# One tap of the feed-forward's convolution scaled by ScalarE and added two tiles at a time, in a hybrid decoder layer

## The chip, the cores and the metric

The kernel runs on one core of one Trainium2 chip. The metric is the device time of one execution in microseconds (us); the time before is the median of three runs. Engines are named as in the profile: PE is TensorE (PEld its weight loads), DVE is VectorE, ACT is ScalarE, POOL is GpSimd, SP issues most DMAs.

## The reference

One decoder layer over 256 tokens and 2048 features, all in float32. Two mixers run side by side on the normed input: a chunked retention with 8 heads, and a gated linear recurrence behind a causal convolution. Their gated sum goes through a projection into the residual stream. Cross-attention to 256 memory tokens (4 heads of 512) follows, then the part that the change touches, and a last norm:

```python
def conv_gated_ffn(hn, w_up, conv_w, conv_b, w_down):
    up = causal_dwconv(hn @ w_up, conv_w, conv_b)      # 3 taps along the tokens, per feature
    gate, val = jnp.split(up, 2, axis=-1)              # 2 x 5632 features
    return (jax.nn.silu(gate) * val) @ w_down
...
        hn = rmsnorm(h, norm_ffn_w[l])
        h = h + conv_gated_ffn(hn, ffn_w_up[l], ffn_conv_w[l], ffn_conv_b[l], ffn_w_down[l])
    return rmsnorm(h, final_norm_w)
```

The convolution is causal: feature by feature, `y[s] = w2*x[s] + w1*x[s-1] + w0*x[s-2] + bias`.

## The kernel before, in words

**Products.** Each float32 product is made of three products of a shorter type (`F32R`): the left side `h + l` and the right side `hi + lo` give `h*hi + l*hi + h*lo`. Weights stream from memory in chunks, in one order for the whole kernel (`weight_plan`, `weight_stream`). ScalarE casts each chunk to `hi` (L451), VectorE subtracts to get `lo` (L452), two chunks ahead of TensorE (`AHEAD = 2`), into rings of six tiles each. L285 is the one line that issues all matmuls.

**Pairs.** `steps_pair` multiplies 256 tokens by two blocks of 512 columns at once, one k-pair (2 x 128 features) per chunk. Two row tiles, two column blocks and two k-tiles make eight products of 512 columns, of three matmuls each. For a k-pair that is *marked* seven products do, after a scheme that multiplies sums of blocks: sums of the weights (`seven_parts`, L473, on VectorE), sums of the token blocks (`sums_of`), and, after the last marked k-pair, a recombination on VectorE (L627) and ScalarE (L620), with three last adds at the pair's end (L638). A pair with no mark is not paired: `weight_plan` turns it into two ordinary products (`gemm_n`).

**MARKS** lists, for each stage and each pair in it, the marked k-pairs. A number below 10 is a marked k-pair whose sums VectorE makes. A number above 20 (22 stands for k-pair 2) is a marked one of which some sums are loaded: `load_twice` brings one block into both halves of a tile `tw`, and `add_to` lets POOL issue a DMA that accumulates two more blocks onto it; VectorE makes two adds that are left (L337). A negative number is no mark: it names a k-pair whose `lo` is made by DMA (tiles `fr` and `fl`; -1 the whole, -11 half of k-pair 1). 

**Order of the work.** Engines work in their own order; a scheduler places instructions, those under `tc.high_priority` early. Work that is to lie beside later products is put off with `later(n, fn)`: `fn` is issued after `n + 1` more chunks. `LAG` holds these numbers by name: `gate` and `value` (the chunks between the end of an up-projection block and its convolution), `key_turn` (the chunks until transposed keys are joined), `sum_load` and `sum_add` (how many chunks ahead the two parts of a loaded sum are issued), `residual` (squares for the norm), `gelu`, `rnn`, `heads`, `squares`, `two_heads` and others. `by_rotate`, `by_conv`, `by_gelu` and `by_attend` choose ScalarE (not 0) or VectorE (0) for the scaling of rows in `turned_rows`.

**The feed-forward.** 11 blocks (0 to 10) of 512 gate and 512 value features: each is a pair of `ffn_w_up` with the gate's and the value's columns. Down-projections stand between them after blocks 4 and 8 and at the end (`ff_plan`). A block's two results are scaled by row on ScalarE (L1421), split into 16-bit planes (L664), transposed by DMA, joined by ScalarE (L677) and then given to `conv` (gate) or `conv` and `gate_up` (value), half of the block's tiles (`pr` 0 or 1) per chunk. `conv` handles a tile of 128 features x 256 tokens: tap 2 and the bias on ScalarE (L1280), taps 1 and 0 as one multiply-add each on VectorE (L1282). `gate_up` applies SiLU (L1290), multiplies (L1291) and splits the result for the down-projection.

Of the kernel before, what the change touches and what calls it, by code (L numbers as in the profile page):

```python
# [13 lines left out]
AF = mybir.ActivationFunctionType  # L14
ALU = mybir.AluOpType
AX = mybir.AxisListType

P = 128
D = 2048
S = 256  # L20
NT = D // P
# [5 lines left out]
FF = 5632  # L27
NF = FF // P
BW = 512
# [5 lines left out]
WARM = 7  # L35
FREE = 300
LAG = dict(
    sums=3, two_heads=3, recur=3, gelu=6, merged=4, memory=1, memory_step=4, rnn=2, rnn_step=2,
    heads=2, heads_step=1, squares=2, squares_step=1, rows=17, rows_step=2, residual=5, gate=2,
    value=4, merge_turn=1, query_turn=2, key_turn=3, turn=3, attend=3, acc_m=0, acc_h=0,  # L40
    by_rotate=0, by_conv=0, by_gelu=1, by_attend=1, far=0, far_load=3, sum_load=4, sum_add=0,
)
EPS = 1e-6
GN_EPS = 1e-5
FF_PARTS = [4, 4, 3]
EARLY = [2, 2, 4, 4, 4]
MARKS = [
# [9 lines left out]
]  # L57

O_Q, O_K, O_V, O_G = 0, 1024, 2048, 4096
O_XR, O_YR, O_GA, O_GB = 6144, 8192, 10240, 12288  # L60
# [139 lines left out]
def hybrid_layer(  # L200
# [17 lines left out]
    act, dve, pe, pool, sp = nc.scalar, nc.vector, nc.tensor, nc.gpsimd, nc.sync  # L218
# [11 lines left out]
    def nm(s):  # L230
        count[0] += 1
        return f"{s}_{count[0]}"

    def big(shape, dt=F32, s="b"):
        return bp.tile(shape, dt, tag="big", name=nm(s))

    def tmp(s="t"):
        return tp.tile([P, 2, S], F32, tag="tmp", name=nm(s))
# [30 lines left out]
    pf = cp.tile([P, 4, NF2], F32, name="pf")  # L269
# [28 lines left out]
    at, scale0, split, far = [0], [], [], {}  # L298
# [181 lines left out]
    def later(n, fn):  # L480

        pending.append((step[0] + n + 1, fn))
# [18 lines left out]
    def ended(steps):  # L501

        for a in steps:
            pass
        return a
# [34 lines left out]
    def gemm_n(*args):  # L540
        return ended(steps_n(*args))
# [98 lines left out]
    def pair(*args):  # L640
        return ended(steps_pair(*args))

    def paired():

        return isinstance(plan[gemms[0]][3], tuple)
# [42 lines left out]
    def turned_rows(a, r, then, wait=1, urgent=True, by=0):  # L688

        rows = big([P, 2, BW], s="rows")  # L690
        with tc.high_priority(FREE) if urgent else nullcontext():
            for tt in range(2):
                scale = act.mul if by else dve.tensor_scalar_mul
                scale(rows[:, tt, :], a[:, tt, :], r[:, tt : tt + 1])  # L694
        by_dma(rows, then, wait)
# [15 lines left out]
    def split_rows(a, r):  # L711

        hi, lo = (big([P, 2, BW], F32R, s="v") for _ in range(2))
        for tt in range(2):
            c = r[:, tt : tt + 1]
            act.mul(hi[:, tt, :], a[:, tt, :], c)
            dve.scalar_tensor_tensor(
                out=lo[:, tt, :], in0=a[:, tt, :], scalar=c, in1=hi[:, tt, :].bitcast(F32),
                op0=ALU.mult, op1=ALU.subtract,
            )  # L720
        return hi, lo
# [78 lines left out]
    xs = Pairs(x_t, p_mix, 1)  # L800
# [9 lines left out]
    rs0 = rstd_rows(ss0)  # L810
# [115 lines left out]
    for g in range(2):  # L926
        dec = big([P, 4, S], s="dec")
        vs, turned = [], ([], [])
        for b, o in enumerate((O_Q, O_K)):

            def rotate_both(f, o=turned[b]):
                o.append(rotated(f[:, 0:2, :]))
                later(0, lambda: o.append(rotated(f[:, 2:4, :])))

            v = None
            if b and not g and paired():
                a, v = pair("w_in", 0, xs, NT, O_K, O_V + BW)
                scaled(a, rs0)
                by_dma(a, rotate_both)
            else:  # L940
                a = gemm_n("w_in", 0, xs, NT, o + g * BW) if g + b else q0
                turned_rows(a, rs0, rotate_both, 2 - b if g + b else 3, g + b > 0, LAG["by_rotate"])
            if b == 1:
                sp.dma_start(
                    out=dec,
                    in_=consts[:, C_DEC + g * 4 * S : C_DEC + (g + 1) * 4 * S].rearrange("p (h s) -> p h s", s=S),
                )
            if g == 0:
                if v is None:
                    v = gemm_n("w_in", 0, xs, NT, O_V + b * BW) if b else ended(v_steps)  # L950
                vs.append(split_rows(v, rs0))
        if g == 1:
            vs += [split_rows(v, rs0) for v in pair("w_in", 0, xs, NT, O_V + 1024, O_V + 1024 + BW)]
        qr, kr = turned
        gates = []
        c = O_G + g * 1024
        for a in pair("w_in", 0, xs, NT, c, c + BW):
            t = big([P, 2, BW], s="gate")
            for tt in range(2):
                act.activation(t[:, tt, :], a[:, tt, :], AF.Silu, scale=rs0[:, tt : tt + 1])  # L960
            gates.append(t)
        retain(g, qr, kr, vs, dec, gates)
# [30 lines left out]
    rnn = []  # L993
# [83 lines left out]
    def tanh_rows(t, a):  # L1077
        for tt in range(2):
            act.activation(t[:, tt, :], a[:, tt, :], AF.Tanh, scale=half_rs0[:, tt : tt + 1])
        return t  # L1080
# [4 lines left out]
    merged, rsms, hrow = [], [], []  # L1085
# [14 lines left out]
    def turn_merged(f):  # L1100
        for pr in range(2):
# [6 lines left out]
            if len(merged) == 2:  # L1108
                for k2 in range(NT // 2):
                    later(LAG["memory"] + LAG["memory_step"] * k2, lambda k2=k2: ms[k2])  # L1110

    ts, mb = [], []
    for b in range(2):
        ts.append(tanh_rows(big([P, 2, BW], s="sig"), gemm_n("w_in", 0, xs, NT, O_GB + b * BW)))
# [2 lines left out]
                later(LAG["rnn"] + LAG["rnn_step"] * i, lambda k2=k2: sums_of(rnn[k2]))  # L1117
    for b in (0, 2):
        if b:
            ts = [tanh_rows(a, a) for a in pair("w_in", 0, xs, NT, O_GB + b * BW, O_GB + (b + 1) * BW)]  # L1120
        for t, z in zip(ts, pair("w_proj_rnn", 0, rnn, NT, b * BW, (b + 1) * BW)):
            gated(t, z)
            mb.append(z)
# [3 lines left out]
        later(LAG["squares"] + LAG["squares_step"] * c, lambda c=c: memory_squares(c))  # L1127
    ts = []
    for b in (0, 2):
        ts += [tanh_rows(a, a) for a in pair("w_in", 0, xs, NT, O_GA + b * BW, O_GA + (b + 1) * BW)]  # L1130
    later(3, memory_begun)
    for b in range(4):
        later(LAG["rows"] + LAG["rows_step"] * b, lambda b=b: hrow.append(load_rows(x, b)))
# [123 lines left out]
    for b, a in enumerate(pair("xa_w_v", 0, ms, NT, 0, BW)):  # L1257
        v = split_rows(a, rsms[0])
        later(LAG["attend"] + b, lambda b=b, v=v: attend(b, v))
    attention(2)  # L1260
    if paired():
        for b, a in enumerate(pair("xa_w_v", 0, ms, NT, 2 * BW, 3 * BW)):
            v = split_rows(a, rsms[0])
            later(LAG["attend"] + b, lambda b=b, v=v: attend(2 + b, v))
    else:
        for b in (2, 3):
            v = split_rows(gemm_n("xa_w_v", 0, ms, NT, b * BW), rsms[0])
            later(1, lambda b=b, v=v: attend(b, v))

    h2s = []  # L1270
    ss2 = residual("xa_w_o", osp, h2s, p_ffn, marks_of("ffn_w_up"))
    rs2 = rstd_rows(ss2)


    def conv(z, t0, dst, pr):

        for j in (2 * pr, 2 * pr + 1):
            t = t0 + j
            y = dst[:, j, :]
            act.activation(y, z[:, j, :], AF.Identity, scale=pf[:, 2, t : t + 1], bias=pf[:, 3, t : t + 1])  # L1280
            for s in range(1, 3):
                dve.scalar_tensor_tensor(  # L1282
                    out=y[:, s:S], in0=z[:, j, 0 : S - s], scalar=pf[:, 2 - s, t : t + 1], in1=y[:, s:S],
                    op0=ALU.mult, op1=ALU.add,
                )

    def gate_up(gt, vl, hid, seven, pr):
        cs = slice(2 * pr, 2 * pr + 2)
# [14 lines left out]
    def down(b0, hid, n):  # L1303

        for b in (0, 2):
            for i, z in enumerate(pair("ffn_w_down", b0 * BW, hid, n, b * BW, (b + 1) * BW)):
                pool.dma_start(out=hrow[b + i], in_=z, accum_op=ALU.add)

    def down_final(b0, hid, n):
# [85 lines left out]
    def up(b, hid, seven, wait):  # L1395

        gt, vl = (big([P, 4, S], s=a) for a in ("fg", "fv"))

        def by_two(fn):
            fn(0)  # L1400
            if b < NF // 4 - 1:
                later(0, lambda: fn(1))
            else:
                fn(1)

        def gate(f):
            by_two(lambda pr: conv(f, 4 * b, gt, pr))

        def value(f):

            def both(pr):
                conv(f, NF + 4 * b, vl, pr)
                gate_up(gt, vl, hid, seven, pr)

            by_two(both)

        two = pair("ffn_w_up", 0, h2s, NT, b * BW, FF + b * BW)
        for a, then, wait in zip(two, (gate, value), (LAG["gate"], wait)):
            with tc.high_priority(FREE):
                for tt in range(2):  # L1420
                    act.mul(a[:, tt, :], a[:, tt, :], rs2[:, tt : tt + 1])  # L1421
            by_dma(a, then, wait)

    hid = {}
    for kind, b, *n in ff_plan():
        if kind == "up":
            b0 = max(one[1] for one in ff_plan() if one[0] == "down" and one[1] <= b)
# [3 lines left out]
        else:  # L1431
            final = b + n[0] == NF // 4
            if final:
                wfin = []
                for i in range(2):
                    t = big([P, 2, BW], s="wf")
                    sp.dma_start(
                        out=t.rearrange("p a n -> p (a n)"),
# [42 lines left out]
```

## Time and profile before

| | us |
|---|---|
| median of three runs | 1955.75 (1953.15 to 1957.33) |
| profiled execution, its own time | 1956.59 |
| its span, first to last instruction | 1954.5 |
| TensorE busy | 1944.4 (99%) |
| VectorE busy | 1659.0 (85%) |
| ScalarE busy | 1457.7 (75%) |
| casts to `hi`, L451 (824) | 801.1 |
| subtractions to `lo`, L452 (824) | 940.4 |

The granted clock of TensorE was 0.999. TensorE's bars overlap, since a matmul's bar (0.39 us for 512 columns) is longer than the distance to the next (0.23 us), and their ends are modelled. The pace is better read from the chain of work that ended last, which lists stretches with their number of matmuls.

### The profile page before, as it was taken

To read this page: it belongs to the slowest core of one execution; us is meant where nothing else is said; L and a number is where in the kernel's file an instruction comes from. 1 tells how busy PE (TensorE), PEld (TensorE's weight loads), DVE (VectorE), ACT (ScalarE), POOL (GpSimd) and SP (SyncE) were. 2 spreads that over 40 slices of the span, in tenths; PEclk is the share of its full clock that TensorE was granted. 3 is DMA by queue.
4 is the path that set the end of the run, shared out by engine and by line. 5 is a ranking of instruction groups with operands and counts; after the bars stand their busy time and mean duration, and the time that the engine had idled before them with its cause. 6 is when DMAs were issued, how large, how long until landed. Compare 5 with 4: busy or idle time off the path is not lost.

```text
span 1954.5 us, 24287 instructions
## 1 busy us (share of the span) xinstructions
PE 1944.4 (99%) x8735; PEld 1612.9 (83%) x8735; DVE 1659.0 (85%) x2155; ACT 1457.7 (75%) x1792; POOL 68.5 (4%) x69
## 2 busy tenths in 40 slices
PE   9999999999999999999999999999999999999998
PEld 7888888888888888888888888888887888888887
DVE  6887987787889988887888857789999889999986
ACT  6665758999756666778678777888877578884784
POOL 0000001000100000000000000000000000000000
PEclk9999999999999999999999999999999999999999
DMA  8866767666867786778868687676677877678773
GB/s 332 262 215 198 245 222 217 213 218 229 237 217 265 233 264 215 253 253 252 247 213 239 223 221 225 226 232 226 211 224 224 269 248 221 223 224 271 230 255 119
DMA packets 211352, 454.99 MB, mean 233 GB/s; under 512 B 143264, under 2 KB 147872, under 8 KB 170400
## 3 DMA queue, kind: packets, MB, share of 16 engines
q1 hardware_dynamic: 204896, 430.38, 66.5%
q0 software_dynamic: 6336, 23.07, 6.3%
q8 instruction: 68, 1.11, 0.2%
q14 instruction: 52, 0.43, 0.1%
HBM read 407.27 MB, written 2.10 MB: 209 GB/s over the span
## 4 chain that ended last, share of the span: by engine, by line
PE 88%; DVE 5%; ACT 3%; DMA 2%; issue 2%; POOL 0%; SPq 0%; POOLq 0%; DVEq 0%; ACTq 0%
PE acc L285 63%; PE sm L285 26%; DVE lo L452 2%; ACT hi L451 1%; DMA raw<-in_wall 1%; ACT f L677 1%; DVE o L627 1%; ACT pl L664 0%; DMA fl<-fr 0%; DVE o L638 0%; DMA pt<-pl 0%; DVE raw L473 0%; DVE fv L1282 0%; DVE fg L1282 0%; DVE s L702 0%
## 5 line engine op out<-in xcount | busy, mean ns | idle before, releaser
L452 DVE TENSOR_TENSOR lo<-raw,hi 128x1024 fp32r<-128x1024 f32 (+1 forms) x824 | 940.4, 1169 | 203.0 <-ACT hi L451 193.0
L285 PE MATMUL acc<-hi,s 128*128 128x512 f32 x3526 | 1081.5, 388 | 0.4 <-ACT s L727 0.2
L451 ACT CAST hi<-raw 128x1024 fp32r<-128x1024 f32 (+1 forms) x824 | 801.1, 1007 | 301.9 <-DMA raw<-in_wall 83.1
L285 PEld LDWEIGHTS acc<-hi,s 128*128 128x128 f32 x3526 | 659.5, 188 | 136.1 <-DVE s L728 0.6
L285 PE MATMUL acc<-lo,s 128*128 128x512 f32 x1727 | 669.7, 388 | 0.1
L285 PE MATMUL sm<-hi,s 128*128 128x512 f32 x1464 | 450.9, 389 | 0.0
L285 PEld LDWEIGHTS acc<-lo,s 128*128 128x128 f32 x1727 | 324.4, 188 | 68.6 <-DVE lo L452 2.1
L285 PEld LDWEIGHTS sm<-hi,s 128*128 128x128 f32 x1464 | 274.7, 188 | 57.2 <-ACT prob L1203 0.2
L285 PE MATMUL sm<-lo,s 128*128 128x512 f32 x720 | 280.3, 389 | 0.0
L677 ACT COPY f<-pt 128x1024 uint16<-128x1024 uint16 x128 | 166.8, 1353 | 10.0 <-DMA pt<-pl 10.0
L285 PEld LDWEIGHTS sm<-lo,s 128*128 128x128 f32 x720 | 135.2, 188 | 28.6 <-DVE lo L452 0.6
L285 PE MATMUL acc<-hi,ts 128*128 128x512 f32 x438 | 134.9, 389 | 0.0
L473 DVE TENSOR_TENSOR raw<-raw 128x1024 f32<-128x1024 f32 x147 | 127.1, 865 | 1.9
L285 PEld LDWEIGHTS acc<-hi,ts 128*128 128x128 f32 x438 | 82.2, 188 | 17.0
L285 PE MATMUL acc<-lo,ts 128*128 128x512 f32 x219 | 85.7, 391 | 0.7 <-DVE lo L452 0.6
L664 ACT COPY pl<-o 128x1024 uint16<-128x1024 uint16 x64 | 62.5, 1040 | 3.7 <-DVE o L638 2.8
L330 POOL DMA_DIRECT2D tw<-in_wall x24 | 21.4, 891 | 980.8 <-DMA tw<-in_wall 355.7
L285 PEld LDWEIGHTS acc<-lo,ts 128*128 128x128 f32 x219 | 41.1, 188 | 10.8 <-DVE lo L452 2.4
L664 ACT COPY pl<-rows 128x1024 uint16<-128x1024 uint16 x44 | 43.7, 1044 | 7.6 <-DVE rows L694 7.6
L1421 ACT ACTIVATE o<-o,ro 128x512 f32<-128x512 f32 x44 | 30.1, 718 | 23.9 <-DVE o L638 23.8
L638 DVE TENSOR_TENSOR o<-o,sm 128x512 f32<-128x512 f32 x64 | 42.2, 679 | 3.9 <-PE sm L285 3.9
L285 PE MATMUL sm<-hi,ts 128*128 128x512 f32 x146 | 45.0, 389 | 0.0
(197 smaller groups left out, 1321.2 us busy)
## 6 DMA issues: line engine op xcount, KB each, us to landing
raw<-in_wall SPq DMA_DIRECT2D x319, 1024.0 KB, 5.1
raw<-in_wall SPq DMA_DIRECT2D x24, 768.0 KB, 5.6
tw<-in_wall SPq DMA_DIRECT2D x24, 512.0 KB, 7.7
tw<-in_wall POOLq DMA_DIRECT2D x24, 512.0 KB, 7.3
raw<-in_wall SPq DMA_DIRECT2D x13, 512.0 KB, 6.6
fr<-in_wall SPq DMA_DIRECT2D x12, 512.0 KB, 7.4
fl<-fr POOLq DMA_DIRECT2D x12, 512.0 KB, 8.1
nat<-in_x SPq DMA_DIRECT2D x8, 512.0 KB, 9.7
```

Of the source, the lines that this page charges most:

```text
L285: tc.keep_in_program_order(pe.matmul(*a, **k))
L330: pool.dma_start(out=far[i], in_=source(i)[:, 0:KH, :], accum_op=ALU.add)
L451: act.copy(hi[:, cs], src[:, cs])
L452: dve.tensor_tensor(out=lo[:, cs], in0=src[:, cs], in1=hi[:, cs].bitcast(F32), op=ALU.subtract)
L473: dve.tensor_tensor(out=o, in0=a, in1=b, op=ALU.add)
L627: dve.tensor_tensor(out=o, in0=a, in1=b, op=op)
L638: dve.tensor_tensor(out=o, in0=o, in1=a, op=ALU.add)
L664: act.copy(planes[:, tt], words[:, tt])
L677: act.copy(halves_[:, :, :, cs], turned_[:, :, :, cs])
L1421: act.mul(a[:, tt, :], a[:, tt, :], rs2[:, tt : tt + 1])
```

## The change

In `conv`, tap 1 is no longer a multiply-add on VectorE. ScalarE scales each tile by tap 1 into a temporary tile `fu`, and one add on VectorE over two tiles (510 elements) puts it, shifted by one token, onto the result. Tap 0 stays a multiply-add.

A helper `blocks` stands where `pair` stood in some places, and yields either a pair's results or those of two ordinary products, so that a pair without marks works there too. It is used where block 10 of the up-projection has no marks now; its rows then go through `turned_rows` (`by_up=0`: VectorE scales).

The marks are set anew: 70 marked k-pairs in place of 73, of which 28 in place of 24 have sums by DMA; three of the halves by DMA (-15 and one -11 in the first recurrent projection, where k-pair 1 is now marked, and -17) are gone. Delays are set anew as well; `sum_add=1` issues the accumulating DMA one chunk earlier.

```diff
 LAG = dict(
-    sums=3, two_heads=3, recur=3, gelu=6, merged=4, memory=1, memory_step=4, rnn=2, rnn_step=2,
-    heads=2, heads_step=1, squares=2, squares_step=1, rows=17, rows_step=2, residual=5, gate=2,
-    value=4, merge_turn=1, query_turn=2, key_turn=3, turn=3, attend=3, acc_m=0, acc_h=0,
-    by_rotate=0, by_conv=0, by_gelu=1, by_attend=1, far=0, far_load=3, sum_load=4, sum_add=0,
+    sums=3, two_heads=2, recur=3, gelu=7, merged=4, memory=1, memory_step=4, rnn=3, rnn_step=1,
+    heads=3, heads_step=2, squares=1, squares_step=0, rows=17, rows_step=2, residual=2, gate=2,
+    value=4, merge_turn=1, query_turn=2, key_turn=5, turn=3, attend=3, acc_m=0, acc_h=0,
+    by_rotate=0, by_conv=0, by_gelu=0, by_attend=4, far=0, far_load=3, sum_load=4, sum_add=1,
+    by_up=0,
 )
 MARKS = [
-    ((), (3, 24, 26), (23,), (3, 4, 26, -11),),
-    ((22, 23, 24, -16, -15, -11), (2, 5, 6, -17, -11), (2, 3, 5),),
-    ((5, 6, 22), (22, 25, 26), (3, 25, 26), (5,),),
+    ((), (3, 24, 26), (23,), (23, 24, 26, -11),),
+    ((1, 22, 24, -16), (2, 5, 6, -11), (22, 23, 25),),
+    ((5, 6, 22), (22, 25, 26), (3, 5, 26), (5,),),
     ((3,), (3, 5),),
-    ((), (5, 23, -6), (2, 3), (2, 5), (2, 5, 23, -1), (),),
+    ((), (5, 23, -6), (2, 3), (2, 5), (22, 23, 25, -1), (),),
     ((22, 25, 26), (),),
     ((2, 4), (2, 5, -1), (3,), (2, 5), (2, 5), (5, 22), (4, 5),),
-    ((3, 22, 24), (2, 5), (4, 22), (4, 5), (2, 5), (4, 22),),
-    ((2, 3, 4, 6), (2, 24), (),),
+    ((2, 23, 24), (2, 5), (22,), (4, 5), (2, 5), (4, 22),),
+    ((2, 3, 4, 6), (), (),),
 ]
@@
+    def blocks(w, row, st, nk, c1, c2):
+
+        if paired():
+            yield from ((a, True) for a in pair(w, row, st, nk, c1, c2))
+        else:
+            for c in (c1, c2):
+                yield gemm_n(w, row, st, nk, c), False
+
@@
     def conv(z, t0, dst, pr):
 
+        cs = slice(2 * pr, 2 * pr + 2)
+        one = tmp("fu")
         for j in (2 * pr, 2 * pr + 1):
             t = t0 + j
-            y = dst[:, j, :]
-            act.activation(y, z[:, j, :], AF.Identity, scale=pf[:, 2, t : t + 1], bias=pf[:, 3, t : t + 1])
-            for s in range(1, 3):
-                dve.scalar_tensor_tensor(
-                    out=y[:, s:S], in0=z[:, j, 0 : S - s], scalar=pf[:, 2 - s, t : t + 1], in1=y[:, s:S],
-                    op0=ALU.mult, op1=ALU.add,
-                )
+            act.activation(
+                dst[:, j, :], z[:, j, :], AF.Identity, scale=pf[:, 2, t : t + 1], bias=pf[:, 3, t : t + 1]
+            )
+            act.mul(one[:, j - 2 * pr, :], z[:, j, :], pf[:, 1, t : t + 1])
+            dve.scalar_tensor_tensor(
+                out=dst[:, j, 2:S], in0=z[:, j, 0 : S - 2], scalar=pf[:, 0, t : t + 1], in1=dst[:, j, 2:S],
+                op0=ALU.mult, op1=ALU.add,
+            )
+        dve.tensor_tensor(out=dst[:, cs, 1:S], in0=one[:, :, 0 : S - 1], in1=dst[:, cs, 1:S], op=ALU.add)
@@
-        two = pair("ffn_w_up", 0, h2s, NT, b * BW, FF + b * BW)
-        for a, then, wait in zip(two, (gate, value), (LAG["gate"], wait)):
+        two = blocks("ffn_w_up", 0, h2s, NT, b * BW, FF + b * BW)
+        for (a, own), then, wait in zip(two, (gate, value), (LAG["gate"], wait)):
+            if not own:
+                turned_rows(a, rs2, then, wait, by=LAG["by_up"])
+                continue
             with tc.high_priority(FREE):
```

Left out above: other places where `pair` becomes `blocks`, all of which keep their pairs.

More of the change, by code (lines that the diff above doesn't have):

```diff
@@ L952, in hybrid_layer @@
         if g == 1:
-            vs += [split_rows(v, rs0) for v in pair("w_in", 0, xs, NT, O_V + 1024, O_V + 1024 + BW)]
+            vs += [split_rows(v, rs0) for v, _ in blocks("w_in", 0, xs, NT, O_V + 1024, O_V + 1024 + BW)]
         qr, kr = turned
@@ L956, in hybrid_layer @@
         c = O_G + g * 1024
-        for a in pair("w_in", 0, xs, NT, c, c + BW):
+        for a, _ in blocks("w_in", 0, xs, NT, c, c + BW):
             t = big([P, 2, BW], s="gate")
@@ L1110, in turn_merged, with tanhs @@
                     later(LAG["memory"] + LAG["memory_step"] * k2, lambda k2=k2: ms[k2])
+    def tanhs(c):
+        for a, own in blocks("w_in", 0, xs, NT, c, c + BW):
+            yield tanh_rows(a if own else big([P, 2, BW], s="sig"), a)
     ts, mb = [], []
@@ L1119, in hybrid_layer @@
         if b:
-            ts = [tanh_rows(a, a) for a in pair("w_in", 0, xs, NT, O_GB + b * BW, O_GB + (b + 1) * BW)]
+            ts = list(tanhs(O_GB + b * BW))
         for t, z in zip(ts, pair("w_proj_rnn", 0, rnn, NT, b * BW, (b + 1) * BW)):
@@ L1129, in hybrid_layer @@
     for b in (0, 2):
-        ts += [tanh_rows(a, a) for a in pair("w_in", 0, xs, NT, O_GA + b * BW, O_GA + (b + 1) * BW)]
+        ts += tanhs(O_GA + b * BW)
     later(3, memory_begun)
@@ L1305, in down @@
         for b in (0, 2):
-            for i, z in enumerate(pair("ffn_w_down", b0 * BW, hid, n, b * BW, (b + 1) * BW)):
+            for i, (z, own) in enumerate(blocks("ffn_w_down", b0 * BW, hid, n, b * BW, (b + 1) * BW)):
+                if not own:
+                    a, z = z, big([P, 2, BW], s="o")
+                    with tc.high_priority(FREE):
+                        act.copy(z, a)
                 pool.dma_start(out=hrow[b + i], in_=z, accum_op=ALU.add)
@@ L1415, in value @@
             by_two(both)
-        two = pair("ffn_w_up", 0, h2s, NT, b * BW, FF + b * BW)
-        for a, then, wait in zip(two, (gate, value), (LAG["gate"], wait)):
+        two = blocks("ffn_w_up", 0, h2s, NT, b * BW, FF + b * BW)
+        for (a, own), then, wait in zip(two, (gate, value), (LAG["gate"], wait)):
+            if not own:
+                turned_rows(a, rs2, then, wait, by=LAG["by_up"])
+                continue
             with tc.high_priority(FREE):
```

## The prediction

> **What bounds the kernel now.** I read the page first, then the waits of TensorE and of its weight loads, then the chain of waits in order of time.
>
> ```profile
> span 1954.5 us, 24287 instructions
> PE 1944.4 (99%) x8735; PEld 1612.9 (83%) x8735; DVE 1659.0 (85%) x2155; ACT 1457.7 (75%) x1792; POOL 68.5 (4%) x69
> ...
> PE acc L285 <- DMA fl<-fr: 0.6, 1, 0.6
> ...
> PEld acc L285 <- DVE lo L452: 4.6, 11, 0.8
> ...
> PEld acc L285 <- DMA fl<-fr: 1.1, 1, 1.1
> ...
> 220.49 5.44 PE sm L285 x24
> ...
> 251.09 6.12 PE acc L285 x27
> ```
>
> TensorE is busy for 1944.4 of 1954.5 us, and a busy bar that is modelled could hide gaps, so the chain decides: 24 matmuls of 512 columns take 5.44 us and 27 take 6.12, both 0.2267 us each, in pieces 30 us apart. Products follow one another at one pace. What interrupts them is small: weight loads waited 4.6 us for `lo` (11 times, at most 0.8) and 1.1 once for a remainder that a DMA makes. So two things move the time: the number of products, and whether the parts of the weights (`hi` cast by ScalarE, `lo` subtracted by VectorE) are there in time. The reserve behind that is thin, which the stretches with the feed-forward's convolution show:
>
> ```profile
> core 0: us, PE busy (x) PEld busy (x) DVE busy (x) ACT busy (x) POOL busy (x), PEclk, DMA share, GB/s
> 1290.00:1503.00 213.00, 212.53 (x933) 174.33 (x932) 195.40 (x269) 181.43 (x224) 0.89 (x1) 1.00 0.69 216
> 1588.00:1756.00 168.00, 168.00 (x743) 139.16 (x742) 156.10 (x213) 145.47 (x179) 1.77 (x2) 1.00 0.73 224
> ```
>
> The first holds five blocks of some 42 us, the second four. VectorE is at 92% and 93%, ScalarE at 85% and 87%. TensorE sets the pace; VectorE is close behind it and ScalarE third.
>
> **The sum's base.** The profiled execution took 1956.59 us (span 1954.5 and 2.1 around it), 0.84 above the median of 1955.75. I sum against 1956.59 and take 0.84 off at the end.
>
> **Fewer seven-product k-pairs: +2.04 us.** A k-pair of a paired product takes 24 matmuls (the 24 of the chain's row), and 21 when it is marked, since one of eight products in three parts each goes. Counting the marks, positive ones only, gives 73 before and 70 after: block 7 of the up-projection loses one and block 10 both of its two, which makes it unpaired. That is 3 x 3 = 9 matmuls more, 9 x 0.2267 = 2.04 us, all on the bounding engine. An unpaired product has as many matmuls as a pair without marks. No cover exists for this term.
>
> **The one DMA wait that goes: -0.8 us.** In the first projection of the recurrent branch the marks -15 and -11 go, and k-pair 1 becomes a plain marked one. The wait stood at its first `fl`:
>
> ```profile
> 511.20 0.62 PE L285 MATMUL sm<-hi,s 128*128 128x512 f32 x2
> ...
> 511.88 0.61 PE L285 MATMUL acc<-hi,s 128*128 128x512 f32 x2
> 513.12 0.50 PE L285 MATMUL acc<-fl,s 128*128 128x512 f32 x1 [0.63 <-DMA fl<-fr]
> ```
>
> Two matmuls that follow at pace end 0.62 us after the first began, so one lasts 0.39 and starts 0.23 after the last: 0.16 of it overlaps. The idle 0.63 therefore cost 0.63 + 0.16 = 0.8. What is late next there is k-pair 1's sums and parts on VectorE; I take nothing for it, since the casts are made two chunks ahead, and bound it at 0.8 lost again.
>
> **Work that VectorE and ScalarE trade outside the convolution: 0.** These are the durations:
>
> ```profile
> L452 DVE TENSOR_TENSOR lo<-raw,hi 128x1024 fp32r<-128x1024 f32 x745 | 889.4, 1220 | 199.5 <-ACT hi L451 189.7 <-PE acc L285 4.2 <-PE sm L285 2.1
> L451 ACT CAST hi<-raw 128x1024 fp32r<-128x1024 f32 x745 | 755.4, 1048 | 273.3 <-DMA raw<-in_wall 80.5 <-PE acc L285 60.6 <-DVE raw L473 45.0
> ...
> L473 DVE TENSOR_TENSOR raw<-raw 128x512 f32<-128x512 f32 x98 | 67.3, 687 | 1.4
> ...
> L473 DVE TENSOR_TENSOR raw<-raw 128x1024 f32<-128x1024 f32 x49 | 59.8, 1219 | 0.5
> ...
> L337 DVE TENSOR_TENSOR raw<-tw,raw 128x512 f32<-128x512 f32 x24 | 16.4, 684 | 0.2
> ...
> L561 ACT CAST ts<-tq 128x512 fp32r<-128x512 f32 x35 | 21.7, 620 | 19.2 <-DVE tq L559 19.1
> ```
>
> A marked k-pair whose sums VectorE makes costs it 1.219 + 2 x 0.687 = 2.59 us of adds. With a sum by DMA two adds of 0.684 stay, 1.37, so each of the sums that becomes a DMA's (24 to 28) frees 1.22, and costs two more transfers of 512 KB, off the path while they land in time. The accumulating transfers are also issued one chunk, 5.44 us, earlier, on POOL's queue, where a marked k-pair now gets its data sooner. Three far halves fewer (a remainder by DMA) put 1.22 each back on VectorE. These edits relieve a VectorE that is not late at most of their places. Their cover is the 42 us of matmuls of each block; if it goes, the price is at most the 4.6 us that weight loads waited for `lo`. A gain has the same bound. I take 0. The moved scalings (`by_gelu`, `by_up`) and the other delays move tens of small operations under the same cover: 0, with the delay of the keys priced below.
>
> **The convolution's tap: +3.9 us.** Per block of the up-projection (8 row tiles, 11 blocks) VectorE ran 16 multiply-adds; now 8 of them and 4 adds over two tiles, and ScalarE runs 8 scalings more.
>
> ```profile
> L1282 DVE SCALAR_TENSOR_TENSOR fg<-f,pf,fg 128x255 f32<-128x255 f32 x44 | 20.4, 479 | 3.1 <-ACT fg L1280 3.0
> ...
> 1482.34 1.66 DVE L1282 SCALAR_TENSOR_TENSOR fg<-f,pf,fg 128x255 f32<-128x255 f32 x4
> ...
> L1291 DVE TENSOR_TENSOR fo<-ft,fv 128x512 f32<-128x512 f32 x22 | 15.0, 682 | 0.0
> ...
> 1096.60 1.28 DVE L627 TENSOR_TENSOR o<-acc,o 128x512 f32<-128x512 f32 x2
> ...
> L727 ACT ACTIVATE s<-f,pb 128x256 fp32r<-128x256 f32 x48 | 21.8, 500 | 0.1
> ...
> 1247.96 0.91 ACT L727 ACTIVATE s<-f,pb 128x256 fp32r<-128x256 f32 x2
> ```
>
> Four multiply-adds in a row take 1.66 with 0.479 for the last: (1.66 - 0.479) / 3 = 0.394 apart. Two adds of 512 take 1.28 with 0.682 for the last: 0.60 apart. VectorE per block: 16 x 0.394 = 6.30 before, 8 x 0.394 + 4 x 0.60 = 5.55 after, so 0.75 less. The nearest row to the new scaling is L727, one column operand and the same 256 elements: 0.50 alone, 0.41 in a row (0.91 - 0.50). I take 0.45, in between, since casts will stand between them: 8 x 0.45 = 3.6 us more per block on ScalarE. So the swap does little of what it looks like: it gives VectorE back 2% of a block and takes 8.5% of it from ScalarE.
>
> Does ScalarE have that? Who it waited for (us in total, times, the longest), five rows of the first stretch, then three of the second:
>
> ```profile
> ACT o L1421 <- DVE o L638: 14.5, 8, 2.7
> ACT hi L451 <- DMA raw<-in_wall: 7.7, 8, 3.0
> ACT hi L451 <- DVE raw L473: 2.8, 4, 1.1
> ACT s L701 <- DVE fo L1291: 2.3, 1, 2.3
> ACT hi L451 <- PE sm L285: 1.3, 3, 0.6
> ...
> ACT o L1421 <- DVE o L638: 5.8, 6, 1.7
> ...
> ACT s L701 <- DVE fo L1291: 3.5, 2, 2.2
> ACT hi L451 <- DVE raw L473: 3.3, 4, 1.9
> ```
>
> First stretch: 213 - 181.4 = 31.6 us idle, of which 14.5 + 2.8 + 2.3 = 19.6 in order behind VectorE; 12.0 are free, and 5 x 3.6 = 18.0 come: 6.0 too much. Second: 168 - 145.5 = 22.5 idle, 5.8 + 3.5 + 3.3 = 12.6 behind VectorE, 9.9 free, and 4 x 3.6 = 14.4 come, less one dropped marked k-pair (casts of 3 x 1.05 + 0.62 in place of 2 x 1.05, and 0.62 for the token sums: 2.3), so 12.1: 2.2 too much; 8.2 together. VectorE's relief (9 x 0.75 = 6.7) shortens waits that are VectorE's, not all of which lie in its new gaps; I credit two thirds, 4.3, leaving 3.9 us of casts that come late. Queued behind the scalings on ScalarE's in-order queue are exactly the `hi` casts; `lo` waits for them, and TensorE for `lo`, as it does 11 times already. The bounds: 0, if the casts' lead swallows it, to 8.2, if the relief is worth nothing.
>
> On the rule: the Trainium skill ("ScalarE: Activation LUTs", section "Rules for kernel authors") gives `mul` and `add` to VectorE and not to ScalarE. This trace agrees for this size: 0.41 to 0.50 for the scaling against 0.394 for a multiply-add that does more. By the rule alone, with no credit for relief, the term is 8.2 and not 3.9.
>
> **Block 10 unpaired: 0.** It loses the pair's recombination and gains two row scalings on VectorE from PSUM; the gate's rows are ready half a block sooner, and the last down-projection needs block 10's rows only in its last chunks. Its cover is that product's first six chunks, 6 x 5.44 = 32.6 us; without it the end would move by what is late.
>
> **Sum.** 1956.59 + 2.04 - 0.8 + 3.9 = 1961.73, less 0.84: **1960.9 us**, 0.26% slower. About 0.2% (3.9 us) is what a measurement of this kernel can tell from no change.
>
> **Rivals.**
> - *The lead absorbs it (not slower by 0.2%).* The ScalarE term is 0: it decides as long as no cast comes later than its lead. For it: ScalarE still waited for TensorE (the 1.3 us row), a cast that is early; and stretches without convolution follow. Against: 12.0 and 9.9 us free against 18.0 and 12.1 wanted. Time: 1956.59 + 2.04 - 0.8 - 0.84 = 1957.0, or down to 1952.4 if all 4.6 us of waits for `lo` go too. Chance 0.30, of which 0.03 below 1951.8, where the other waits of TensorE would have to shrink as well.
> - *No credit for VectorE's relief.* Time: 1956.59 + 2.04 - 0.8 + 8.2 - 0.84 = 1965.2; the rule above points here. For it: VectorE's longest waits are for ScalarE's casts (189.7 us). Against: its own lateness is what 19.6 of ScalarE's idle 31.6 us are. Chance 0.15.
> - *Keys late.* The second keys' joins come two chunks, 10.9 us, later, and the last split of these keys ended at 1088.52 + 0.68 = 1089.2, with the products of the logits from 1102.33:
>
> ```profile
> 1088.52 0.68 DVE L702 TENSOR_TENSOR s<-f,s 128x512 fp32r<-128x512 f32 x1
> ...
> 1102.33 1.84 PE L285 MATMUL sm<-s,s 128*128 128x256 f32 x14
> ```
>
>   13.1 us of slack become 2.2. A queue 2.2 us longer makes TensorE wait, up to another chunk: 1960.9 + 5.4 = 1966.3. Chance 0.05, since the join needs only its two copies and two splits.
>
> **Chances.** Forecast 0.50 (0.45 of it above 1959.7, 0.05 below), lead absorbs 0.30, no credit 0.15, keys 0.05. Slower 0.45 + 0.15 + 0.05 = 0.65; same 0.05 + 0.27 = 0.32; faster 0.03. The range runs from 1956, below the absorbed case by its noise, to 1967.5, above the last two rivals; in the likeliest case alone 1958.5 to 1963.5.
>
> **What would show it.** Matmuls 8735 + 9 = 8744 on the page at 0.2267 us each; no `fl` wait near 512; ScalarE near 94% between 1290 and 1756, VectorE near 90%; the wait of weight loads for `lo` up from 4.6 to about 8 us, nearly all at marked k-pairs of blocks 1 to 9. The forecast is wrong if those waits stay under 5 us, or if the excess lies ahead of the feed-forward, where I put nothing.

## The result, and the profile after

The changed kernel took 1959.76 us (median of 8 runs, 1956.78 to 1961.28), the kernel before 1954.9 in 8 runs beside it: ratio 1.0022, 95% interval 1.0011 to 1.0032. In a second job it took 1956.99 us (11 runs, 1956.09 to 1963.58) against 1955.08: 1.0016, 1.0007 to 1.0024. The ratio is taken over all runs and is not the quotient of the two medians, which is 1.0025 and 1.0010. The changed kernel is slower, by 0.16 to 0.22% by the ratios, a size at the edge of what can be told from no change. Its profiled execution took 1958.56 us, 1.97 more than that of before; the medians lie 4.9 us apart in the first job and 1.9 in the second, so single waits are read below from the profiles, and costs from the medians.

The page of the changed kernel, then the two stretches with the convolution (same columns as before):

```profile
span 1956.8 us, 24371 instructions
...
PE 1945.7 (99%) x8744; PEld 1615.6 (83%) x8744; DVE 1645.1 (84%) x2105; ACT 1477.4 (76%) x1859; POOL 68.1 (3%) x70
```

```profile
1290.00:1503.00 213.00, 212.92 (x939) 175.96 (x939) 195.45 (x253) 197.64 (x266) 1.76 (x2) 1.00 0.70 218
1588.00:1756.00 168.00, 166.50 (x724) 136.62 (x724) 146.04 (x186) 152.98 (x206) 1.74 (x2) 0.99 0.72 222
```

TensorE has the 9 matmuls more that were counted, 8744. In the first stretch ScalarE went from 181.4 to 197.6 of 213 us, 93%, near the 199.4 worked out, and TensorE waits no more there for it: it was busy for 212.92 us, against 212.53 before. In the second TensorE's bars leave 1.5 us of 168 open. The groups of the new convolution in the changed kernel, and for whom its weight loads waited over the whole span:

```profile
L1298 ACT ACTIVATE fu<-f,pf 128x256 f32<-128x256 f32 x88 | 43.8, 500 | 0.0
...
L1299 DVE SCALAR_TENSOR_TENSOR fg<-f,pf,fg 128x254 f32<-128x254 f32 x44 | 20.4, 480 | 7.5 <-ACT fg L1295 7.5
...
L1303 DVE TENSOR_TENSOR fg<-fu,fg 128x510 f32<-128x510 f32 x22 | 15.2, 689 | 1.4
```

```profile
PEld acc L286 <- DVE lo L453: 2.3, 4, 1.3
PEld acc L286 <- ACT hi L452: 1.2, 2, 0.9
PEld sm L286 <- DVE lo L453: 1.2, 2, 0.7
PEld sm L286 <- issue: 1.1, 1, 1.1
```

A scaling lasts 0.500 us, as its nearest row did, and an add over two tiles 0.689. (`acc` and `sm` are two kinds of accumulators of matmuls.) The waits for `lo` into `acc` fell from 4.6 us (11) to 2.3 (4), those into `sm` rose from 0.6 to 1.2, and the wait for `fl` is gone. What is left of the waits for `hi` and `lo` stands mostly in one place, the marked k-pairs 4 and 5 of block 8, here in the timeline of TensorE:

```profile
1696.68 0.73 PE L286 MATMUL acc<-hi,s 128*128 128x512 f32 x2
1697.40 0.50 PE L286 MATMUL acc<-lo,s 128*128 128x512 f32 x1
1698.52 0.73 PE L286 MATMUL acc<-hi,ts 128*128 128x512 f32 x2 [0.61 <-ACT hi L452]
1700.14 0.66 PE L286 MATMUL acc<-lo,ts 128*128 128x512 f32 x1 [0.89 <-DVE lo L453]
1700.59 1.05 PE L286 MATMUL acc<-hi,ts 128*128 128x512 f32 x2
1701.44 0.63 PE L286 MATMUL acc<-lo,ts 128*128 128x512 f32 x1
```

Before, no weight load waited anywhere between 1588 and 1756. Here the starts are 1.12 us apart over one matmul and 1.62 over two, where the pace is 0.23 and 0.45. Measured against the pace, 4.1 us go between 1696 and 1704: 2.4 up to the start at 1700.14, and 1.7 because the nine matmuls from there on come 0.43 us apart.

That is not a net loss of 4.1 us. Added up over the whole profile, the steps from one 512-column matmul to the next that are longer than the pace (by over 0.025 us) lose 6.0 us before, all of it ahead of 1690, and 6.7 in the changed kernel, 2.6 of it ahead of 1690. So this execution shows the 9 matmuls and 0.7 us of waits more. The medians of the first job lie further apart than that; where those executions lost the rest was not profiled.

The wait for the remainder at 512 had lost 0.9 us by this measure. A new one of 0.9 stands at 231, in the first k-pair of the retention's second gates, far ahead of the feed-forward; it ends with VectorE's last adds (L639):

```profile
231.12 0.70 PE L286 MATMUL sm<-hi,s 128*128 128x512 f32 x2 [0.69 <-DVE o L639]
```

### The profile page after: what moved, and what is told of

Its sections match the earlier page's. It is cut to its first block, busy times and chain, and to the rows that moved or that the text cites. A ratio compares the mean times of both kernels' runs of the same rounds, so it can differ in the third digit from the quotient of the medians.

```text
span 1956.8 us, 24371 instructions
## 1 busy us (share of the span) xinstructions
PE 1945.7 (99%) x8744; PEld 1615.6 (83%) x8744; DVE 1645.1 (84%) x2105; ACT 1477.4 (76%) x1859; POOL 68.1 (3%) x70
## 4 chain that ended last, share of the span: by engine, by line
PE 94%; ACT 2%; DVE 2%; DMA 1%; issue 1%; POOL 0%; POOLq 0%; DVEq 0%; ACTq 0%
PE acc L286 67%; PE sm L286 27%; DMA raw<-in_wall 1%; ACT hi L452 1%; DVE lo L453 1%; DMA pt<-pl 0%; ACT f L686 0%; ACT fu L1298 0%; ACT fv L1295 0%; DMA raw<-in_head 0%; DVE o L639 0%; ACT ft L1308 0%; ACT fg L1295 0%; DVE tb L858 0%; ACT o L1446 0%
## 5 line engine op out<-in xcount | busy, mean ns | idle before, releaser
L286 PE MATMUL acc<-hi,s 128*128 128x512 f32 (+1 forms) x3596 | 1102.2, 388 | 0.3 <-ACT s L736 0.3
L286 PEld LDWEIGHTS acc<-hi,s 128*128 128x128 f32 x3596 | 672.4, 188 | 138.1 <-ACT s L736 0.5
L286 PE MATMUL acc<-lo,s 128*128 128x512 f32 (+1 forms) x1774 | 687.4, 388 | 0.0
L286 PE MATMUL sm<-hi,s 128*128 128x512 f32 x1424 | 438.5, 389 | 0.7 <-DVE o L639 0.7
L286 PEld LDWEIGHTS acc<-lo,s 128*128 128x128 f32 x1774 | 333.1, 188 | 69.0 <-DVE lo L453 0.4
L286 PEld LDWEIGHTS sm<-hi,s 128*128 128x128 f32 x1424 | 267.1, 188 | 56.5 <-issue 1.1
L286 PE MATMUL sm<-lo,s 128*128 128x512 f32 x700 | 272.6, 389 | 0.3 <-DVE lo L453 0.2
L474 DVE TENSOR_TENSOR raw<-raw 128x512 f32<-128x512 f32 (+1 forms) x126 | 109.2, 867 | 1.7
L639 DVE TENSOR_TENSOR o<-o,sm 128x512 f32<-128x512 f32 x62 | 40.7, 683 | 6.7 <-PE sm L286 6.6
L562 ACT CAST ts<-tq 128x512 fp32r<-128x512 f32 x36 | 22.4, 621 | 29.2 <-DVE tq L560 29.1
L1298 ACT ACTIVATE fu<-f,pf 128x256 f32<-128x256 f32 x88 | 43.8, 500 | 0.0
```

The lines of the kernel that those rows point to most:

```text
L286: tc.keep_in_program_order(pe.matmul(*a, **k))
L474: dve.tensor_tensor(out=o, in0=a, in1=b, op=ALU.add)
L562: act.copy(o[:, 0], s)
L639: dve.tensor_tensor(out=o, in0=o, in1=a, op=ALU.add)
L1298: act.mul(one[:, j - 2 * pr, :], z[:, j, :], pf[:, 1, t : t + 1])
```

## The experiments

The question after the result: are the 3 to 5 us the 9 matmuls and ScalarE's lateness, as forecast, or something else? Each time stands beside runs of the kernel before on the same chip. Block numbers are those of the up-projection.

**The convolution alone.** `conv` of the changed kernel in the kernel before.

```diff
-            for s in range(1, 3):
-                dve.scalar_tensor_tensor(out=y[:, s:S], ...)
+            act.mul(one[:, j - 2 * pr, :], z[:, j, :], pf[:, 1, t : t + 1])
...
+        dve.tensor_tensor(out=dst[:, cs, 1:S], in0=one[:, :, 0 : S - 1], in1=dst[:, cs, 1:S], op=ALU.add)
```

> The kernel before with the new convolution alone (tap 1 scaled by ScalarE, one add over two tiles); marks and delays as before. Theory (late casts because ScalarE has no room): about 3 to 4 us slower than before, 1958 to 1959 against 1954.9, with more waiting of weight loads for lo in blocks 1 to 9. Rival (the casts' lead absorbs the scalings): within 1 us of before; the 4.9 us between the two kernels then lie in marks (2.0) and delays (2.9).

1955.54 us against 1955.65: ratio 1.0001 (0.9993 to 1.0010), so between 1.4 us less and 2.0 more. The theory falls, the rival's time holds (that the delays cost the rest does not, as the old marks show below). The two stretches, and ScalarE's waits in the first, show why:

```profile
1290.00:1503.00 213.00, 213.00 (x941) 176.28 (x940) 195.72 (x254) 198.26 (x266) 1.76 (x2) 1.00 0.70 220
1588.00:1756.00 168.00, 166.92 (x737) 137.90 (x736) 153.12 (x196) 154.84 (x210) 2.63 (x3) 1.00 0.73 225
```

```profile
ACT o L1425 <- DVE o L638: 8.1, 7, 2.2
ACT hi L451 <- DMA raw<-in_wall: 3.2, 3, 1.9
ACT hi L451 <- DVE raw L473: 1.8, 2, 1.1
```

ScalarE worked 16.8 us more and waited less: for VectorE's last adds of a pair 8.1 us in place of 14.5, for loads 3.2 in place of 7.7. It came later to places where it would have waited anyway. No weight load waited in that stretch; before, they waited 2.7 us there, all for `lo`. Two other places lose time against the pace where before lost none: 1.4 us at 1753, for `lo`, and 1.5 at 1913, where the last down-projection needs block 10's tiles:

```profile
PEld acc L285 <- DVE s L702: 0.9, 1, 0.9
PEld acc L285 <- ACT s L701: 0.8, 1, 0.8
```

Over the whole profile 4.8 us are lost, and 6.0 before: in these two executions the scalings moved waits and did not add any.

**The old convolution in the changed kernel.** The same edit turned round.

> The changed kernel with the old convolution put back (taps 1 and 0 on VectorE); new marks and delays stay. Theory: 3 to 4 us faster than the changed kernel, 1956 to 1957 against 1959.8. Rival: unchanged at 1959 to 1960, or slower if VectorE needed the relief.

1958.11 us, 1.0016 (1.0007 to 1.0024). That is the changed kernel's second ratio to the digit, and 1.65 us under its first median; no cost of the convolution can be told here either, and 3 to 4 us are excluded by the experiment before.

**Three marks taken away.** Before, with block 7's k-pair 4 and both of block 10 unmarked (which needs `blocks`).

```diff
-    ((3, 22, 24), (2, 5), (4, 22), (4, 5), (2, 5), (4, 22),),
-    ((2, 3, 4, 6), (2, 24), (),),
+    ((3, 22, 24), (2, 5), (22,), (4, 5), (2, 5), (4, 22),),
+    ((2, 3, 4, 6), (), (),),
```

> The kernel before with only the three marks taken away that the change drops (k-pair 4 of block 7, both of block 10, which is then unpaired); old convolution, old delays, all other marks old. Both theories: 9 matmuls more at 0.2267 us, so 2.0 us slower than before, 1956.9; less, down to 0, only if the work that these marks cost VectorE and ScalarE made TensorE wait.

1958.58 us, 1.0018 (1.0009 to 1.0027): 2.9 us more, the 2.0 of the matmuls and perhaps some more. With the old convolution and old delays the wait at block 8 is there, in three parts (TensorE's timeline):

```profile
1699.89 0.50 PE L286 MATMUL acc<-lo,ts 128*128 128x512 f32 x1 [0.53 <-DVE lo L453]
...
1701.62 0.73 PE L286 MATMUL acc<-hi,ts 128*128 128x512 f32 x2 [0.53 <-ACT hi L452]
1703.02 0.50 PE L286 MATMUL acc<-lo,ts 128*128 128x512 f32 x1 [0.66 <-DVE lo L453]
```

So neither the scalings nor the new delays are needed for it. Of the three marks it is the one of block 7 that decides, as the runs with block 7's and with block 10's marks put back show below.

**The old delays in the changed kernel.** `LAG` as before, `by_up=0` added.

> The changed kernel with all delays as before (the choice of engine for the gelu rows included); new convolution and new marks stay. Theory (delays cost nothing): the time of the changed kernel, 1959 to 1960.5. Rival (the delays cost 2.9 us): about 1957.

1963.12 us (6 runs, 1960.15 to 1971.22), 1.0043 (1.0029 to 1.0057): slower than the changed kernel, not equal and not faster. Its profile shows TensorE waiting once for a remainder made by DMA, in the second gates of the retention, the pair whose marks became (23, 24, 26, -11):

```profile
PE acc L286 <- DMA fl<-fr: 2.6, 1, 2.6
```

Against the pace 4.5 us go there, between 236 and 241. So the new marks need the new delays. That the third loaded sum of that pair holds the remainder's DMA up is likely but not shown, and which of the delays prevents it was not tried.

**All 73 old marks in the changed kernel.** What stays of the change is the new convolution and the new delays.

> The changed kernel with all 73 marks of before: new convolution and new delays alone. Theory (the marks carry the loss; convolution and delays cost nothing): 1954.5 to 1956, the time before. Rival (the new delays fit the new marks only): 2 us or more slower than before.

1955.34 us, 0.9999 (0.9990 to 1.0008). With the old marks the whole loss is gone, so neither the new convolution nor the new delays cost anything by themselves. No weight load waits for `fl` here either, though the marks -15 and -11 are back: the new delays alone take away the wait at 512.

**Block 7's mark put back; block 8's marks moved apart.** Two edits of the changed kernel, each of one number.

```diff
-    ((2, 23, 24), (2, 5), (22,), (4, 5), (2, 5), (4, 22),),
+    ((2, 23, 24), (2, 5), (4, 22), (4, 5), (2, 5), (4, 22),),      # first kernel
+    ((2, 23, 24), (2, 5), (22,), (2, 5), (2, 5), (4, 22),),        # second kernel
```

> The changed kernel with the one mark of block 7 put back (k-pair 4), block 10 still unpaired. Theory A (without that mark the scheduler sets block 7's end so that the casts for the two neighbouring marked k-pairs of block 8 come some 3 us late): the stall near 1700 is gone, 0.7 us of matmuls are gone, so about 4 us faster than the changed kernel, 1955.5 to 1956.5. Rival B (the scalings on ScalarE make that stall): the stall stays, only the 0.7 us go, 1959.

1958.17 us, 1.0014 (1.0005 to 1.0023).

> The changed kernel with one mark of block 8 moved from k-pair 4 to 2, so that its two marked k-pairs (now 2 and 5) are no longer neighbours; as many matmuls. Theory A: the stall near 1700 is gone, 3 to 4 us faster than the changed kernel, 1956 to 1957. Rival C (any block 8 is late behind this block 7): the stall stays at k-pair 5, 1959 to 1960.

1957.62 us, 1.0011 (1.0002 to 1.0020), 2.2 us over before: about the 2.0 that 9 matmuls cost at 0.2267. Its only wait of a weight load between 1588 and 1756 is this:

```profile
PEld sm L286 <- DVE lo L453: 0.4, 1, 0.4
```

In both profiles the wait at block 8 is gone. In time the expected 3 to 4 us did not come: 1.6 and 2.1 us below the first median of the changed kernel, and above its second one. The profiles suggest why: other waits stand in its place, one between 1750 and 1760 in the first kernel (1.7 us against the pace), two rows of them between 1480 and 1502 in the second (2.7):

```profile
PEld acc L286 <- DVE lo L453: 1.8, 1, 1.8
```

```profile
PEld acc L286 <- DVE lo L453: 1.6, 2, 1.1
PEld sm L286 <- DVE lo L453: 1.5, 1, 1.5
```

Over the whole profile the two lose 5.2 and 6.2 us against the pace, the changed kernel 6.7 and, in a second profile, 4.8.

**The changed kernel again, and block 10's marks put back.**

> The changed kernel once more, on the chip of the next two. Theory (9 matmuls more, 2.0 us, and a stall of 2 to 4 us at the two neighbouring marked k-pairs of block 8): 1958.5 to 1960.5, with TensorE waiting near 1700 in this profile too. Rival (that stall was a chance of one execution): about 1957.5 and no wait there.

1956.99 us, as told above. The wait is there again, but shorter (between 1680 and 1712):

```profile
PEld acc L286 <- DVE lo L453: 1.8, 2, 1.3
PEld acc L286 <- ACT hi L452: 0.3, 1, 0.3
```

It loses 1.7 us. So the theory's place holds and its size does not: the median lies at the rival's 1957.5 or below.

```diff
-    ((2, 3, 4, 6), (), (),),
+    ((2, 3, 4, 6), (2, 24), (),),
```

> The changed kernel with the two marks of block 10 put back, the one of block 7 still gone. Theory: 6 matmuls fewer, 1.4 us faster than the changed kernel, and the stall near 1700 stays: 1958 to 1959. Rival (the dropped mark of block 7 does not make that stall): 1956.

1958.64 us, 1.0021 (1.0012 to 1.0030); 1.65 above the changed kernel beside it and not 1.4 below, a difference that runs spread over 8 us do not settle. The wait near 1700 stayed, 1.3 us. The 6 matmuls fewer, 1.4 us, are paid back at one place: 1.3 us go at 1914, in two waits of 0.9 and 0.6 us for block 10's tiles, like those of the convolution alone. The four kernels with one scaling a tile and block 10 marked (convolution alone, old marks, this one, more marks) lose 1.3 to 1.5 us there. Those with block 10 unmarked, or with the old convolution, lose nothing there. With the new convolution, taking block 10's marks away was therefore about even.

Over all profiles, the time lost against TensorE's pace near 1700 was 4.1, 1.7, 2.9, 3.3, 1.7 and 1.3 us in the six with block 7 at (22,) and block 8 at (4, 5): the changed kernel twice, old convolution, three marks less, old delays and block 10 back. It was nothing in six others: before, convolution alone, old marks, block 7 back, block 8 apart, and the kernel that follows.

**More marks.** The kernel with old marks, new convolution and new delays has room, it seemed, for three marks more.

```diff
-    ((3,), (3, 5),),
+    ((3, 25), (3, 5),),
...
-    ((5, 6, 22), (22, 25, 26), (3, 25, 26), (5,),),
+    ((5, 6, 22), (22, 25, 26), (3, 25, 26), (23, 5),),
...
-    ((), (5, 23, -6), (2, 3), (2, 5), (2, 5, 23, -1), (),),
+    ((), (5, 23, -6), (2, 3, 25), (2, 5), (2, 5, 23, -1), (),),
```

> The new convolution and the new delays with the 73 marks of before and three more where VectorE and ScalarE have room: k-pair 5 (a loaded sum) in the first half of the mixers' output projection, 3 (loaded) in the second half of the retention's projection, 5 (loaded) in the second queries. 9 matmuls fewer than before: 2.0 us, 1953.4 against 1955.4, if the casts still come in time; rival (each new mark makes a stall where its sums are late): 1955 or more.

1960.41 us, 1.0033 (1.0021 to 1.0046): the rival. There are 9 matmuls fewer, and in the stretch from 780 to 840 alone, with two of the new marks, these waits of weight loads:

```profile
PEld acc L286 <- DVE lo L453: 4.8, 7, 1.3
```

Against the pace 4.1 us go there, and 2.0 more at 984, in the pair of the third new mark, for sums of the token blocks (`ts`). A mark is worth 0.68 us only where its sums are in time.

**How much ScalarE can take.** The convolution alone, with each scaling made twice, then with every second one made twice (into the same place).

```diff
+            for _ in range(2):              # second kernel: range(2 - j % 2)
                 act.mul(one[:, j - 2 * pr, :], z[:, j, :], pf[:, 1, t : t + 1])
```

> The kernel before with the new convolution, and each scaling of tap 1 made twice into the same place, so that ScalarE gets another 0.41 us per tile, 3.3 us per block. With one scaling ScalarE was busy 198.3 of 213 us between 1290 and 1503 at no loss of time. If what decides is whether its work fits under the matmuls: 198.3 + 5 x 3.3 = 214.8 and about 10 us of waits do not fit into 213, so 8 to 20 us slower than before over the 11 blocks. If the lead and the rows without convolution absorb this as well: within 2 us of before.

1983.28 us, 1.0143 (1.0129 to 1.0157), 27.9 us more: the first reading, and beyond its 8 to 20.

> The kernel before with the new convolution, and the scaling of every second tile made twice: one and a half times the scalings, 5 us per block on ScalarE. With one dose nothing was lost, with two 27.9 us. Theory E (all of ScalarE's 31.6 us of idle time between 1290 and 1503 can be filled, because it waits less for VectorE the later it comes): 5 x 5.0 = 25 us fit, so at most 3 us slower than before. Rival (only the 12 us that were not waits behind VectorE can be filled and the lead hides the first dose): the loss is about in the middle, 10 to 16 us.

1968.34 us, 1.0068 (1.0054 to 1.0082), 12.6 us more: theory E falls, at least as a bound on the sum over a stretch, and the loss lies in the rival's 10 to 16. The waits of weight loads for `lo` in the kernels with no scaling, one, one and a half, and two:

```profile
PEld acc L285 <- DVE lo L452: 4.6, 11, 0.8
```

```profile
PEld acc L285 <- DVE lo L452: 2.2, 3, 1.5
```

```profile
PEld acc L285 <- DVE lo L452: 8.2, 8, 2.0
PEld acc L285 <- ACT s L701: 4.3, 2, 3.0
```

```profile
PEld acc L285 <- DVE lo L452: 16.1, 15, 3.1
```

The first dose is free, and from there the loss is steep. The 4.3 us of the third kernel begin at 1918, where the last down-projection needs block 10's tiles: there both halves of the convolution are issued at once, and nothing later can catch up. Of the time this kernel loses against the pace, 7.7 us go there, about 2.4 of them (an estimate: twelve matmuls, 0.2 each) because the matmuls came at half the pace; 5.4 go between 1290 and 1503.

Two readings of the free first dose remain: waits behind VectorE that shrink, or the casts' lead. The shrinking is measured; that the lead had no part in it is not.

## Why the prediction was right, and where it was not

The time, 1959.76, was forecast at 1960.9, and 0.22% slower at 0.26%. That it came so near is luck: the largest term of the sum measured nothing, and the second job's 1956.99 is the time of the rival that the lead absorbs the scalings (1957.0). Point by point:

- *Fewer marks, +2.04.* Right, and the only part of the sum that is shown in time: 8744 matmuls, 2.2 us for the kernel with block 8's marks apart, where that wait is gone, and nothing lost at all once the old marks are back.
- *The remainder's wait, -0.8.* It is gone as forecast, and k-pair 1's parts came in time, but the reason given is not the only one: under the new delays it is gone with the old marks too. And the changed kernel loses as much, 0.9 us, at 231. The other place where a remainder can come late, 236 under the old delays, cost 4.5 us and was not thought of.
- *Work traded outside the convolution and delays, 0.* Right for the pair that was made, wrong as an argument: delays and marks are not each worth nothing. With the new marks and the new convolution, the old delays cost 2.6 to 5.6 us more than the new (7.5 over before, against 4.9 and 1.9).
- *The convolution's tap, +3.9.* Wrong: it measured nothing (1.0001, at most 2.0 us). ScalarE's new busy time was about right, 197.6 us against 199.4 worked out. The step that failed is "19.6 in order behind VectorE; 12.0 are free": it took ScalarE's waits for a fixed cost that new work is added to. In the run those for VectorE's last adds shrank as ScalarE came later (14.5 to 8.1 us): they are a distance between two queues, as far as this shows. All 31.6 us were not free either, as half a dose more showed. The rival "the lead absorbs it", at 0.30, was right about the size of this term.
- *In its place:* waits that the marks make, above all one of 1.3 to 4.1 us where block 8's two neighbouring marked k-pairs meet the end of block 7. The prediction costed the mark of block 7 as three matmuls and did not ask what its neighbours' casts would do. In the kernel before, the last `lo` there ended at 1701.86, only 0.26 us ahead of a weight load that waits for VectorE. How taking a mark away makes the next block's casts later stays open: in the kernel with three marks less ScalarE waited 2.2 us for VectorE's last add of block 7 (1.5 before) ahead of those casts, but in the changed kernel 1.2, so this wait does not explain it.
- *Keys late, block 10 unpaired:* no wait at either place in the changed kernel. Block 10's 0 leaves out that its marks and the new convolution together make a wait of 1.3 to 1.5 us, about what its 6 matmuls cost.
- *The test that was set*, waits for `lo` near 8 us, and "wrong if they stay under 5", came out wrong: 3.5 us into `acc` and `sm` together, less than the 5.2 before. Sign and size came out right in sum, with the tap's 3.9 too much in it and the marks' waits missing. How much of the 1.9 to 4.9 us beyond the 2.0 these waits are stays open: the edits that remove the one at block 8 gained 1.6 and 2.1 us by one median and nothing by the other, and the profile of the changed kernel loses only 0.7 us more in waits than that of before.

The rule named in the prediction is that of the Trainium skill ("ScalarE: Activation LUTs", "Rules for kernel authors"): `mul` and `add` go to VectorE. For one operation this trace agrees, by little: 0.50 us for a bare scaling on ScalarE, 0.48 for a multiply-add on VectorE. In this kernel, scaling on ScalarE cost nothing that could be measured at one scaling a tile, and 27.9 us at two.

## What to carry to other kernels

Idle time of an in-order engine that waits behind another is partly room. In this kernel, work put there cost nothing until the engine came later than those it had waited for, and then it cost most of its own length: 44 scalings more, 18 us at 0.41 each by estimate, cost 12.6 us, and 88 cost 27.9. The largest single loss stood where nothing follows that could catch up. So a dose of the work made one and a half and two times tells more than the sum of busy times. When the bounding engine's work is cut by a trick that feeds on the other engines, count each use at its place: three uses less cost what they saved or a little more (2.9 us, of which 2.0 are matmuls), three uses more cost five microseconds. And add up the lost time over the whole profile: a wait that goes at one place can come back at another.

## What the runs showed of the hardware

After some waits TensorE went on at half its pace for a few microseconds. In the changed kernel the waits of 0.61 and 0.89 us (1698 to 1700) were followed by matmuls 0.43 us apart until 1704. The granted clock was 0.89 over the 16 us around them and 0.50 inside:

```profile
1690.00:1706.00 16.00, 14.50 (x54) 10.74 (x54) 15.10 (x20) 15.97 (x23) 0.00 (x0) 0.89 0.36 133
1700.40:1703.60 3.20, 3.20 (x9) 2.43 (x9) 3.20 (x4) 3.20 (x5) 0.00 (x0) 0.50 0.20 44
```

The second profile of the same kernel has the wait and not the slow stretch, and loses 1.7 us there in place of 4.1. The kernel with the old delays has such a stretch after its wait of 2.6 us, and that with one and a half scalings after one of 2.5:

```profile
237.60:240.80 3.20, 3.20 (x9) 2.52 (x8) 3.20 (x6) 1.60 (x3) 0.00 (x0) 0.50 1.01 400
```

```profile
1922.50:1929.00 6.50, 5.04 (x12) 3.16 (x11) 3.51 (x4) 1.86 (x3) 0.00 (x0) 0.50 0.41 125
```

In the kernel with three marks less, waits of 0.53, 0.53 and 0.66 us at the same place were not followed by that (clock 1.00 between 1690 and 1706), nor was one of 2.7 us in the kernel with two scalings, at 1731. So a wait can cost more than it shows, here 4.1 us for 1.5 of idle time; where the line runs these profiles do not tell.
